# The first two w_ada sections of a hybrid decoder block: from ScalarE and GpSimd to TensorE

## The chip, the cores and the metric

The kernel runs on one NeuronCore of one Trainium2 chip. The metric is the device time of one execution in microseconds (us). Engines are named as the profile names them: PE is TensorE (PEld its weight loads), DVE is VectorE, ACT is ScalarE, POOL is GpSimd, SP the queue that issues most DMAs.

## The reference

One decoder layer on 512 tokens of width 2048, in float32, conditioned on one vector c:

```python
mod = jax.nn.silu(c) @ w_ada[l] + b_ada[l]              # (2048) @ (2048 x 12288)
sh1, sc1, g1, sh2, sc2, g2 = jnp.split(mod, 6, axis=-1)
u = _modulate(_rmsnorm(h, norm_attn[l]), sh1, sc1)      # rmsnorm(h) * (1 + sc1) + sh1
y = _hybrid_mixer(u, ...)                               # z = u @ w_in, attention, w_out
h = h + g1[:, None, :] * y
u = _modulate(_rmsnorm(h, norm_ffn[l]), sh2, sc2)
h = h + g2[:, None, :] * _swiglu(u, w_gate[l], w_up[l], w_down[l])
```

Nothing of `u @ w_in` can start for a block of channels before sh1 and sc1 of those channels are there. They are the first two of the six sections of `mod`, two products of SiLU(c) with 2048 x 2048 matrices.

## The kernel before, in words

All big products are made of pairs of fp32r numbers, high and low part, as three matmuls (`mm_ws`, L253 to L255: high by high, high by low, low by high) with 512 columns streamed. Weights come in chunks of two 128-row blocks; `fetch_w` (L221) loads one, ACT makes the high half `wh` (L237) and DVE or POOL the low half `wl` (L238).

The change lies in the early stage, the loop `while step < SLOTS + 8 or todo` (from L472). It forms sc1 and sh1 and at once uses them. The two sections are cut into 8 passes jj of 256 columns. A pass has two keys (k2 = 0 is section 1, the scale; k2 = 1 is section 0, the shift), and a key has four tiles `ad` of 512 rows by 256 columns (four row blocks q), one DMA each (L478) into 8 buffers. So there are 64 tiles, and tile n is loaded at step n. One step of the loop records, in this order: the DMA of tile `step`; the products of tile `step - 1` with SiLU(c), kept as a column per row block in `sl`; and, for the tile n that `due(step, what)` names (only the last of a pass), the sum over partitions (what = 0), `mod` and the first half of the modulation (what = 1), and its second half (what = 2). `LAGS` sets how many steps after n each comes: 3, 4 and 5, in the last pass 2, 3 and 4. Then two or three entries of `todo` are taken, each a unit of three L253 to L255 matmuls; a pass adds 14 units in the first half of the stage and 22 in the second. Each engine runs its own instructions in the recorded order.

Before the change the products of a tile are shared so: DVE multiplies and adds two or three of the four row blocks into `acc` (L490, L492), ACT multiplies the others (L497, L500), and POOL adds ACT's results into `acc2` (L501). The sum over partitions is a matmul with the 128 x 128 block of `acc` as weights and a column of ones streamed (L509), into a bank `sums`. DVE adds the bias (`mod`, L518), makes `a_vec` (L370) and `mt` (L384), ACT makes `uh` (L386), DVE makes `ul` (L390). `uh` and `ul` are what L253 to L255 stream.

In the same stage POOL makes two `wl` per pass (L238); in the second half DVE makes the `wl` for the key and value columns (index i = 1), recorded at step 2 of the next pass. DVE also computes rotary tables (L400 to L420), one instruction a step from step 6.

Of the kernel before, what the change touches and what calls it, by code (L numbers as in the profile page):

```python
# [9 lines left out]
F32 = mybir.dt.float32  # L10
F32R = mybir.dt.float32r
I32 = mybir.dt.int32
AF = mybir.ActivationFunctionType
OP = mybir.AluOpType
AX = mybir.AxisListType

P = 128
# [8 lines left out]
EPS = 1e-6  # L26
ADW = 8
LAG = 2
LAGS = (3, 4, 5), (2, 3, 4)
R_C, R_D, R_F, R_V = 1.0, 1.0, 1.0, 0.6  # L30
SCALE = HD ** -0.5
NCMP = 31
# [45 lines left out]
def hymba_block(ctx: ExitStack, tc: tile.TileContext, x, c, positions, w_ada, b_ada, norm_attn,  # L78
                norm_ffn, w_in, b_fgate, cmp_pos, w_kc1, w_kc2, w_vc1, w_vc2, beta_fox, beta_nsa,
                w_out, w_gate, w_up, w_down, final_norm, cst, out):  # L80
    nc = tc.nc
# [5 lines left out]
    def pool(stack, name, bufs=1, **kw):  # L87
        return stack.enter_context(tc.tile_pool(name=name, bufs=bufs, **kw))
# [18 lines left out]
    def bank(tag, shape=(P, T)):  # L107
        return ps.tile(list(shape), F32, tag=tag, name=uid("ps" + tag), bufs=SETS[tag])
# [6 lines left out]
    ident = cs[:, K_ID:K_ID + P]  # L115
    one_col = cs[:, K_ONE:K_ONE + 1]
# [4 lines left out]
    early = pool(st, "early")  # L121
# [23 lines left out]
    sl = con.tile([P, ND], F32, name="sl")  # L145
# [34 lines left out]
    for t in range(NT):  # L180
        for g in range(4):
# [9 lines left out]
            else:  # L191
                nc.vector.scalar_tensor_tensor(junk, src, 1.0, src, op0=OP.mult, op1=OP.mult,
                                               accum_out=ssq4[:, t, g:g + 1])
# [9 lines left out]
    b_mod = vec[:, 0:96]  # L203
# [5 lines left out]
    mod = con.tile([P, 96], F32, name="mod")  # L209
# [222 lines left out]
    NJ = ND // 2  # L432
    HJ = NJ // 2

    def w_pairs(j):
        s1 = fetch_w(p_s1, j, src=early, width=3 * P, bufs=2)
        if j < HJ:
            return [fetch_w(p_qn, j), s1]
        i = 2 * (j - HJ)
        return [fetch_w(p_cmp, i), s1, fetch_w(p_cmp, i + 1)]  # L440
# [17 lines left out]
    xsp = dram.tile([ND, P, T], F32, name="xsp")  # L458
    SLOTS = 8 * NJ

    def due(step, what):
        for n in range(7, SLOTS, 8):
            if step == n + LAGS[n == SLOTS - 1][what]:
                return n

    def on_dve(n):
        return n % 2 == 0

    tiles, accs, accs2, sums, halves, fetched, todo = {}, {}, {}, {}, {}, {}, []
    extra_work = tables()  # L470
    step = 0
    while step < SLOTS + 8 or todo:  # L472
        j, r = divmod(step, 8)
        if j < NJ:
            sec, q0 = (1, 0)[r // 4], 4 * (r % 4)
            tiles[step] = early.tile([P, 4, 256], F32, tag="adw", name=uid("ad"), bufs=ADW)
            c0 = sec * D + j * 256
            nc.sync.dma_start(tiles[step], w_ada[:, c0:c0 + 256].rearrange("(q p) n -> p q n", p=P)[:, q0:q0 + 4, :])  # L478
        if r == 2 and j < NJ:
            fetched[j] = w_pairs(j)  # L480
        n = step - 1
        if 0 <= n < SLOTS:
            key, q0 = n // 4, 4 * (n % 4)
            if q0 == 0:
                accs[key] = early.tile([P, 256], F32, tag="acc", name=uid("acc"), bufs=3)
            acc = accs[key]
            for q in (0, 1, 3) if on_dve(n) else (0, 1):
                sc1 = sl[:, q0 + q:q0 + q + 1]
                if q0 + q == 0:
                    nc.vector.tensor_scalar(acc, tiles[n][:, q, :], sc1, None, op0=OP.mult)  # L490
                else:
                    nc.vector.scalar_tensor_tensor(acc, tiles[n][:, q, :], sc1, acc, op0=OP.mult, op1=OP.add)  # L492
            for q in (2,) if on_dve(n) else (2, 3):
                sc1 = sl[:, q0 + q:q0 + q + 1]
                if q0 + q == 2:
                    accs2[key] = early.tile([P, 256], F32, tag="acc2", name=uid("acc2"), bufs=3)
                    nc.scalar.activation(accs2[key], tiles[n][:, q, :], AF.Copy, scale=sc1)  # L497
                else:
                    tm = early.tile([P, 256], F32, tag="tm", name=uid("tm"), bufs=2)
                    nc.scalar.activation(tm, tiles[n][:, q, :], AF.Copy, scale=sc1)  # L500
                    nc.gpsimd.tensor_tensor(accs2[key], accs2[key], tm, op=OP.add)  # L501
        n = due(step, 0)
        if n is not None:
            jj = n // 8
            sums[jj] = bank("mm")
            for k2 in range(2):
                for av in (accs, accs2):
                    for i in range(2):
                        nc.tensor.matmul(sums[jj][:, 2 * k2 + i:2 * k2 + i + 1],  # L509
                                         av[2 * jj + k2][:, i * P:(i + 1) * P], one_col,  # L510
                                         start=k2 == 0 and av is accs and i == 0,
                                         stop=av is accs2, skip_group_check=True)
        n = due(step, 1)
        if n is not None:
            jj = n // 8
            for k2, sec in ((0, 1), (1, 0)):
                m0 = sec * ND + 2 * jj
                nc.vector.tensor_tensor(mod[:, m0:m0 + 2], sums[jj][:, 2 * k2:2 * k2 + 2], b_mod[:, m0:m0 + 2],  # L518
                                        op=OP.add)
            scale_vec(0, jj * 2, 2)  # L520
            pend = [modulate_a(0, i, xT[:, i, :], rstd1, early) for i in (2 * jj, 2 * jj + 1)]
        n = due(step, 2)
        if n is not None:
            u.extend([modulate_b(*h) for h in pend])
            jj = n // 8
            if jj < HJ:
                todo += units(halves[jj][0], jj, S0, ND // 2)
            if jj == HJ - 1:
                todo.append(keep_half)
            todo += units(halves[jj][1], jj, S1, ND)  # L530
        for _ in range(2 if step < 8 * HJ + LAGS[0][2] else 3):
            if todo:
                todo.pop(0)()
        if 0 < j <= NJ and r % 2 == 0 and r // 2 < len(fetched[j - 1]):
            i = r // 2
            w = fetched[j - 1][i](nc.vector if i == 1 and j > HJ else nc.gpsimd)
            halves.setdefault(j - 1, []).append(w)
            pr = 2 * (j - 1 - HJ) + i // 2
            if j > HJ and i != 1:
                todo += units(w, pr, S0, ND)  # L540
        if step >= 6:
            next(extra_work, None)
        step += 1
# [378 lines left out]
    for pr in range(4):  # L922
# [4 lines left out]
        for i in range(2):  # L927
            q = pair("q", 6, "qf")
# [166 lines left out]
```

## Time and profile before

| what | value |
|---|---|
| median of three runs | 2519.67 us |
| lowest and highest run | 2519.4 and 2530.77 us |
| the profiled execution: its time, its span | 2530.77 us, 2530.7 us |
| instructions | 29434 |
| PE busy | 2408.5 us (95%), 11475 matmul records |
| DVE, ACT, POOL busy | 1253.7, 775.3, 231.9 us |
| HBM over the span | 133 GB/s |
| early stage | first 214 us of the span |

The profile lists, for the whole span and for any stretch of it, how long each engine was busy, each instruction's start and duration, what ended the idle time before it, and the TensorE clock that was granted (1.00 is 2.4 GHz, 0.50 is 1.2 GHz). A float32 matmul has two records in the trace, an fp32r matmul one; a matmul's duration includes its way through the array, so the pace of a chain is read from start to start.

### The profile page before, as it was taken

To read this page: it belongs to the slowest core of one execution; us is meant where nothing else is said; L and a number is where in the kernel's file an instruction comes from. 1 tells how busy PE (TensorE), PEld (TensorE's weight loads), DVE (VectorE), ACT (ScalarE), POOL (GpSimd) and SP (SyncE) were. 2 spreads that over 40 slices of the span, in tenths; PEclk is the share of its full clock that TensorE was granted. 3 is DMA by queue.
4 is the path that set the end of the run, shared out by engine and by line. 5 is a ranking of instruction groups with operands and counts; after the bars stand their busy time and mean duration, and the time that the engine had idled before them with its cause. 6 is when DMAs were issued, how large, how long until landed. Compare 5 with 4: busy or idle time off the path is not lost.

```text
span 2530.7 us, 29434 instructions
## 1 busy us (share of the span) xinstructions
PE 2408.5 (95%) x11475; PEld 2005.5 (79%) x11475; DVE 1253.7 (50%) x1978; ACT 775.3 (31%) x1221; POOL 231.9 (9%) x204
## 2 busy tenths in 40 slices
PE   4688999999999989999999999999999999999998
PEld 3576887788888768788888888888888888888887
DVE  8995786887755565565423323223323233322233
ACT  4443543434423332232222222222122222122233
POOL 5463000200010220000000000000000000000011
PEclk7798999999999999999999999999999999999999
DMA  9782654454644266456532333332333333233332
GB/s 301 226 275 77 187 151 125 124 156 114 189 149 150 86 206 226 149 175 191 159 100 92 100 96 96 100 94 97 100 92 100 98 93 100 96 96 100 93 99 100
DMA packets 226794, 339.02 MB, mean 134 GB/s; under 512 B 17648, under 2 KB 102480, under 8 KB 226656
## 3 DMA queue, kind: packets, MB, share of 16 engines
q1 hardware_dynamic: 223376, 332.46, 43.0%
q10 hardware_dynamic: 2304, 4.20, 0.4%
q8 instruction: 90, 1.47, 0.2%
q0 software_dynamic: 976, 0.50, 0.1%
q14 instruction: 48, 0.39, 0.1%
HBM read 324.45 MB, written 12.65 MB: 133 GB/s over the span
## 4 chain that ended last, share of the span: by engine, by line
PE 60%; DMA 2%; DVE 1%; issue 0%; ACT 0%; SPq 0%; POOLq 0%; POOL 0%; ACTq 0%; DVEq 0%
PE psmm L253 10%; PE psmm L255 10%; PE psmm L254 10%; PE pss L255 7%; PE pss L253 7%; PE pss L254 7%; PE pso L254 2%; PE pso L253 2%; PE pso L255 2%; DMA wr<-in_w_out_dram 1%; DMA ad<-in_w_ada_dram 1%; DVE acc L356 0%; DVE wl L238 0%; PE psmm L819 0%; ACT wh L237 0%
## 5 line engine op out<-in xcount | busy, mean ns | idle before, releaser
L238 DVE TENSOR_TENSOR wl<-wr,wh 128x1024 fp32r<-128x1024 f32 (+2 forms) x370 | 433.6, 1172 | 966.7 <-ACT wh L237 965.1
L237 ACT CAST wh<-wr 128x1024 fp32r<-128x1024 f32 (+2 forms) x386 | 384.5, 996 | 1199.5 <-PE pso L254 521.7
L253 PE MATMUL psmm<-uh,wh 128*128 128x512 f32 x1010 | 401.0, 398 | 11.9 <-ACT uh L386 5.7
L254 PE MATMUL psmm<-ul,wh 128*128 128x512 f32 x1010 | 398.3, 394 | 2.0 <-DVE ul L390 2.0
L255 PE MATMUL psmm<-uh,wl 128*128 128x512 f32 x1010 | 398.4, 395 | 1.3 <-DVE wl L238 1.3
L253 PE MATMUL pss<-uh,wh 128*128 128x512 f32 x600 | 238.9, 398 | 17.8 <-ACT uh L386 17.8
L254 PE MATMUL pss<-ul,wh 128*128 128x512 f32 x600 | 238.5, 398 | 5.2 <-DVE ul L390 5.2
L255 PE MATMUL pss<-uh,wl 128*128 128x512 f32 x600 | 237.9, 397 | 1.0 <-POOL wl L238 0.9
L253 PEld LDWEIGHTS psmm<-uh,wh 128*128 128x128 f32 x1010 | 192.2, 190 | 54.5 <-ACT uh L386 6.8
L356 DVE SCALAR_TENSOR_TENSOR acc<-ad,sl,acc 128x512 f32<-128x512 f32 x240 | 187.7, 782 | 94.8 <-DMA ad<-in_w_ada_dram 92.2
L255 PEld LDWEIGHTS psmm<-uh,wl 128*128 128x128 f32 x1010 | 192.4, 190 | 43.6 <-DVE wl L238 2.4
L254 PEld LDWEIGHTS psmm<-ul,wh 128*128 128x128 f32 x1010 | 192.2, 190 | 41.7 <-DVE ul L390 3.0
L992 POOL TENSOR_TENSOR fsum<-fsum,sq 128x512 f32<-128x512 f32 x13 | 19.4, 1492 | 1452.7 <-ACT sq L990 1452.0
L253 PEld LDWEIGHTS pss<-uh,wh 128*128 128x128 f32 x600 | 115.3, 192 | 43.9 <-ACT uh L386 19.7
L254 PEld LDWEIGHTS pss<-ul,wh 128*128 128x128 f32 x600 | 115.3, 192 | 31.0 <-DVE ul L390 7.0
L253 PE MATMUL psmm<-fh,wh 128*128 128x512 f32 x352 | 136.9, 389 | 0.0
L254 PE MATMUL psmm<-fl,wh 128*128 128x512 f32 x352 | 136.9, 389 | 0.0
L255 PE MATMUL psmm<-fh,wl 128*128 128x512 f32 x352 | 136.9, 389 | 0.0
L255 PEld LDWEIGHTS pss<-uh,wl 128*128 128x128 f32 x600 | 115.2, 192 | 26.0 <-POOL wl L238 1.8
L492 DVE SCALAR_TENSOR_TENSOR acc<-ad,sl,acc 128x256 f32<-128x256 f32 x144 | 111.2, 772 | 4.8 <-DMA ad<-in_w_ada_dram 0.5
L253 PE MATMUL pss<-fh,wh 128*128 128x512 f32 x264 | 102.7, 389 | 0.0
L254 PE MATMUL pss<-fl,wh 128*128 128x512 f32 x264 | 102.7, 389 | 0.0
(373 smaller groups left out, 4050.8 us busy)
## 6 DMA issues: line engine op xcount, KB each, us to landing
ad<-in_w_ada_dram SPq DMA_DIRECT2D x192, 512.0 KB, 4.4
wr<-in_w_gate_dram SPq DMA_DIRECT2D x88, 512.0 KB, 3.7
wr<-in_w_up_dram SPq DMA_DIRECT2D x88, 512.0 KB, 3.7
wr<-in_w_down_dram SPq DMA_DIRECT2D x88, 512.0 KB, 3.7
wr<-in_w_in_dram SPq DMA_DIRECT2D x104, 256.0 KB, 3.7
wr<-in_w_in_dram SPq DMA_DIRECT2D x24, 512.0 KB, 4.6
wr<-in_w_out_dram SPq DMA_DIRECT2D x24, 512.0 KB, 4.8
wr<-in_w_in_dram SPq DMA_DIRECT2D x48, 128.0 KB, 3.0
```

Source lines behind the costliest of these rows:

```text
L237: nc.scalar.copy(wh[:, :, s], v)
L238: lo.tensor_tensor(wl[:, :, s], v, split_ap(wh)[:, :, s], op=OP.subtract)
L253: nc.tensor.matmul(dst, wh[:, k, w], ah, start=first, stop=False)
L254: nc.tensor.matmul(dst, wh[:, k, w], al, start=False, stop=False)
L255: nc.tensor.matmul(dst, wl[:, k, w], ah, start=False, stop=last)
L356: nc.vector.scalar_tensor_tensor(acc, wr[:, q, :], s, acc, op0=OP.mult, op1=OP.add)
L492: nc.vector.scalar_tensor_tensor(acc, tiles[n][:, q, :], sc1, acc, op0=OP.mult, op1=OP.add)
L992: nc.gpsimd.tensor_tensor(acc[0], acc[0], sq, op=OP.add)
```

## The change

ACT and POOL no longer take part in the products. DVE keeps its share (three row blocks of an even tile, two of an odd one), and PE takes the rest: the column of `sl` is repeated to a 128 x 128 block of weights, past which 256 float32 columns of the tile are streamed (L498), so that every row of the result holds the same sums. DVE's `acc` joins by a product with a block of ones (L501). All go into one bank `rows` with two halves, used by the keys in turn. DVE multiplies each 128 columns of it with the identity and sums along the row, which picks the diagonal into a column (`dj`, L508). The sums over partitions (L509) go. `LAGS` becomes 2, 3 and 4 for every pass; the PE products are due every step, the picks after every key.

```diff
-LAGS = (3, 4, 5), (2, 3, 4)
+LAGS = 2, 3, 4
...
-    def due(step, what):
-        for n in range(7, SLOTS, 8):
-            if step == n + LAGS[n == SLOTS - 1][what]:
-                return n
-
-    def on_dve(n):
-        return n % 2 == 0
-
-    tiles, accs, accs2, sums, halves, fetched, todo = {}, {}, {}, {}, {}, {}, []
+    def due(step, what, every=8):
+        n = step - LAGS[what]
+        return n if 0 <= n < SLOTS and n % every == every - 1 else None
+
+    def n_dve(n):
+        return 3 - n % 2
+
+    tiles, accs, halves, fetched, todo = {}, {}, {}, {}, []
+    rows = bank("mm", (P, 2, 256))
+    diag = early.tile([P, 2 * NJ, 2], F32, name="diag")
...
-            for q in (0, 1, 3) if on_dve(n) else (0, 1):
+            for q in range(n_dve(n)):
...
-            for q in (2,) if on_dve(n) else (2, 3):
-                sc1 = sl[:, q0 + q:q0 + q + 1]
-                if q0 + q == 2:
-                    accs2[key] = early.tile([P, 256], F32, tag="acc2", name=uid("acc2"), bufs=3)
-                    nc.scalar.activation(accs2[key], tiles[n][:, q, :], AF.Copy, scale=sc1)
-                else:
-                    tm = early.tile([P, 256], F32, tag="tm", name=uid("tm"), bufs=2)
-                    nc.scalar.activation(tm, tiles[n][:, q, :], AF.Copy, scale=sc1)
-                    nc.gpsimd.tensor_tensor(accs2[key], accs2[key], tm, op=OP.add)
-        n = due(step, 0)
+        n = due(step, 0, 1)
         if n is not None:
-            jj = n // 8
-            sums[jj] = bank("mm")
-            for k2 in range(2):
-                for av in (accs, accs2):
-                    for i in range(2):
-                        nc.tensor.matmul(sums[jj][:, 2 * k2 + i:2 * k2 + i + 1],
-                                         av[2 * jj + k2][:, i * P:(i + 1) * P], one_col,
...
+            key, q0 = n // 4, 4 * (n % 4)
+            for q in range(n_dve(n), 4):
+                nc.tensor.matmul(rows[:, key % 2, :], sl[:, q0 + q:q0 + q + 1].to_broadcast([P, P]),
+                                 tiles[n][:, q, :], start=n % 4 == 0 and q == n_dve(n), stop=False)
+            if n % 4 == 3:
+                nc.tensor.matmul(rows[:, key % 2, :], one_col.to_broadcast([P, P]), accs[key],
+                                 start=False, stop=True)
+        n = due(step, 1, 4)
+        if n is not None:
+            key = n // 4
+            for i in range(2):
+                dj = early.tile([P, P], F32, tag="dj", name=uid("dj"), bufs=2)
+                nc.vector.scalar_tensor_tensor(dj, rows[:, key % 2, i * P:(i + 1) * P], 1.0, ident, op0=OP.mult,
+                                               op1=OP.mult, accum_out=diag[:, key, i:i + 1])
...
-                nc.vector.tensor_tensor(mod[:, m0:m0 + 2], sums[jj][:, 2 * k2:2 * k2 + 2], b_mod[:, m0:m0 + 2],
-                                        op=OP.add)
+                nc.vector.tensor_tensor(mod[:, m0:m0 + 2], diag[:, 2 * jj + k2, :], b_mod[:, m0:m0 + 2], op=OP.add)
```

How the instructions stand now, first on PE at the end of a pass in the second half of the stage. Before, the sums over partitions stand in one group, and the units follow (`pss`, `pso` and `psmm` are banks of units, `psmm` with L509 the bank `sums`):

```order
L509 MATMUL psmm_1224<-cs,acc_1008 128x1 [waits PE_49]
L509 MATMUL psmm_1224<-cs,acc_1008 128x1
L509 MATMUL psmm_1224<-cs,acc_228_1012 128x1 x2
L509 MATMUL psmm_1224<-cs,acc_1119 128x1 [waits DVE_49]
L509 MATMUL psmm_1224<-cs,acc_1119 128x1
L509 MATMUL psmm_1224<-cs,acc_253_1123 128x1 x2
L253 MATMUL pso_976<-uh_745,wh_1186 128x512
```

Now, at the same place (`psmm_286` is `rows`, `ad_908` the second tile of the next pass, `uh_947` and `ul_948` the first channels of the finished pass):

```order
L498 MATMUL psmm_286<-ad_908,sl 128x256 [waits DMAHW3_49,DVE_49]
L498 MATMUL psmm_286<-ad_908,sl 128x256
L253 MATMUL pss_872<-uh_392,wh_904 128x512
L254 MATMUL pss_872<-ul_393,wh_904 128x512
L255 MATMUL pss_872<-uh_392,wl_905 128x512
L253 MATMUL pso_873<-uh_392,wh_904 128x512
L254 MATMUL pso_873<-ul_393,wh_904 128x512
L255 MATMUL pso_873<-uh_392,wl_905 128x512
L253 MATMUL psmm_282<-uh_947,wh_964 128x512 [waits Activation_49]
L254 MATMUL psmm_282<-ul_948,wh_964 128x512 [waits DVE_49]
L255 MATMUL psmm_282<-uh_947,wl_965 128x512
L498 MATMUL psmm_286<-ad_926,sl 128x256 [waits DMAHW4_49]
```

The products of a tile now stand between the units, ahead of the units of every step, and one in four steps' products waits for DVE; the product of the first tile of that pass stands ten rows ahead of this piece, with three units between.

On DVE, the same place, before (`acc_1373` is the next pass's accumulator, `wl_1424` the low half of the key and value columns):

```order
L238 TENSOR_TENSOR wl_1424<-wr_1209,wh_1423 128x768 [waits Activation_49]
L492 SCALAR_TENSOR_TENSOR acc_1373<-ad_1388,sl,acc_1373 128x256 [waits DMAHW4_49,DVE_49]
L492 SCALAR_TENSOR_TENSOR acc_1373<-ad_1388,sl,acc_1373 128x256 [waits DVE_49] x2
L518 TENSOR_TENSOR mod<-psmm_1405,vec 128x2 [waits PE_49]
L518 TENSOR_TENSOR mod<-psmm_1405,vec 128x2
L370 SCALAR_TENSOR_TENSOR a_vec<-mod,vec 128x2 [waits DVE_49]
L384 SCALAR_TENSOR_TENSOR mt_1438<-xT,a_vec,rstd_269 128x512 [waits DVE_49]
L384 SCALAR_TENSOR_TENSOR mt_1443<-xT,a_vec,rstd_269 128x512
L492 SCALAR_TENSOR_TENSOR acc_1373<-ad_1427,sl,acc_1373 128x256 [waits DMAHW1_49]
L492 SCALAR_TENSOR_TENSOR acc_1373<-ad_1427,sl,acc_1373 128x256 [waits DVE_49]
L390 SCALAR_TENSOR_TENSOR ul_1441<-mt_1438,mod,uh_1440 128x512 [waits Activation_49]
```

And now:

```order
L508 SCALAR_TENSOR_TENSOR dj_938,diag<-psmm_286,cs 128x128 [waits PE_49]
L508 SCALAR_TENSOR_TENSOR dj_940,diag<-psmm_286,cs 128x128
L515 TENSOR_TENSOR mod<-diag,vec 128x2
L515 TENSOR_TENSOR mod<-diag,vec 128x2 [waits DVE_49]
L370 SCALAR_TENSOR_TENSOR a_vec<-mod,vec 128x2 [waits DVE_49]
L384 SCALAR_TENSOR_TENSOR mt_945<-xT,a_vec,rstd_269 128x512 [waits DVE_49]
L384 SCALAR_TENSOR_TENSOR mt_950<-xT,a_vec,rstd_269 128x512
L238 TENSOR_TENSOR wl_965<-wr_778,wh_964 128x768 [waits Activation_49]
L493 SCALAR_TENSOR_TENSOR acc_910<-ad_926,sl,acc_910 128x256 [waits DMAHW4_49]
L493 SCALAR_TENSOR_TENSOR acc_910<-ad_926,sl,acc_910 128x256 [waits DVE_49] x2
L390 SCALAR_TENSOR_TENSOR ul_948<-mt_945,mod,uh_947 128x512
```

The two picks stand ahead of `mod`, and `wl` and three instead of two products stand between `mt` and `ul`, since the modulation is recorded one step earlier while `wl` stays at its step.

## Rows read from the trace of the kernel before

**Rows 1.** The page's busy times, and a late stretch by windows (us; PEclk, DMA share, GB/s).

```profile
PE 2408.5 (95%) x11475; PEld 2005.5 (79%) x11475; DVE 1253.7 (50%) x1978; ACT 775.3 (31%) x1221; POOL 231.9 (9%) x204
...
300.00:2530.00 2230.00, 2183.99 (x10418) 1820.16 (x10416) 1008.88 (x1605) 641.56 (x974) 99.48 (x81) 0.99 0.41 123
```

**Rows 2.** Windows of the eight passes and the tail: PE, PEld, DVE, ACT, POOL busy, PEclk.

```profile
22.00:46.30 24.30, 5.97 (x24) 5.42 (x24) 22.95 (x37) 9.62 (x19) 15.05 (x15) 0.50 1.09 351
46.30:70.50 24.20, 16.53 (x58) 12.84 (x58) 23.67 (x36) 8.52 (x16) 13.95 (x12) 0.71 0.68 216
70.50:93.90 23.40, 14.70 (x58) 11.25 (x58) 22.87 (x34) 10.95 (x19) 13.56 (x12) 0.72 0.78 249
93.90:114.10 20.20, 15.09 (x58) 11.67 (x58) 19.56 (x29) 8.51 (x16) 12.89 (x12) 0.78 0.79 241
114.10:136.00 21.90, 19.16 (x72) 15.12 (x73) 20.22 (x31) 9.47 (x18) 10.67 (x11) 0.79 0.52 166
136.00:157.50 21.50, 20.44 (x93) 16.09 (x92) 20.90 (x29) 9.36 (x17) 13.44 (x12) 0.98 0.92 286
157.50:179.00 21.50, 18.79 (x82) 15.29 (x82) 20.90 (x30) 9.35 (x17) 13.41 (x12) 0.92 0.84 266
179.00:196.50 17.50, 13.06 (x60) 10.74 (x60) 15.37 (x20) 6.91 (x12) 10.96 (x9) 0.95 0.85 311
196.50:214.00 17.50, 17.50 (x66) 13.84 (x65) 8.27 (x13) 7.16 (x11) 6.67 (x4) 0.85 0.23 75
```

**Rows 3.** Groups of the early stage: line, engine, count, busy us, mean ns, idle before.

```profile
L492 DVE SCALAR_TENSOR_TENSOR acc<-ad,sl,acc 128x256 f32<-128x256 f32 x144 | 111.2, 772 | 4.8 <-DMA ad<-in_w_ada_dram 0.5
L501 POOL TENSOR_TENSOR acc<-acc,tm 128x256 f32<-128x256 f32 x80 | 68.4, 857 | 83.2 <-ACT tm L500 79.2
...
L500 ACT ACTIVATE tm<-ad,sl 128x256 f32<-128x256 f32 x80 | 38.6, 503 | 32.4 <-POOL acc L501 30.3 <-DMA ad<-in_w_ada_dram 1.7
...
L509 PE MATMUL psmm<-cs,acc 128*128 128x1 f32 x128 | 18.8, 270 | 21.2 <-DVE acc L492 20.0 <-POOL acc L501 1.2
```

**Rows 4.** Timelines of DVE and POOL, 140 to 160 us: start, us, what, count.

```profile
141.05 11.19 DVE L492 SCALAR_TENSOR_TENSOR acc<-ad,sl,acc 128x256 f32<-128x256 f32 x9
...
155.85 1.52 DVE L492 SCALAR_TENSOR_TENSOR acc<-ad,sl,acc 128x256 f32<-128x256 f32 x3
...
140.83 2.45 POOL L238 TENSOR_TENSOR wl<-wr,wh 128x1024 fp32r<-128x1024 f32 x1
143.23 4.45 POOL L501 TENSOR_TENSOR acc<-acc,tm 128x256 f32<-128x256 f32 x5
```

**Rows 5.** Timelines of PE: a unit's pace, and float32 products with a repeated column.

```profile
144.39 0.39 PE L255 MATMUL pss<-uh,wl 128*128 128x512 f32 x1
144.62 0.39 PE L253 MATMUL pss<-uh,wh 128*128 128x512 f32 x1
...
822.09 1.05 PE L171 MATMUL pss<-cs,rsnr 128*128 128x128 f32 x8
822.90 0.36 PE L258 MATMUL psmm<-wh,uh 128*128 128x256 f32 x1
```

**Rows 6.** Timeline of DVE, beginning and end of its work: a PSUM copy, the last modulation, POOL beside it.

```profile
20.22 0.28 DVE L199 COPY vec<-pss 128x128 f32<-128x128 f32 x1
...
196.31 0.23 DVE L518 TENSOR_TENSOR mod<-psmm,vec 128x2 f32<-128x2 f32 x2 [1.74 <-PE psmm L509]
...
199.63 0.96 DVE L238 TENSOR_TENSOR wl<-wr,wh 128x768 fp32r<-128x768 f32 x1 [1.51 <-ACT wh L237]
200.50 3.54 DVE L390 SCALAR_TENSOR_TENSOR ul<-mt,mod,uh 128x512 fp32r<-128x512 f32 x2
...
200.62 2.88 POOL L238 TENSOR_TENSOR wl<-wr,wh 128x1024 fp32r<-128x1024 f32 x1 [7.38 <-ACT wh L237]
```

**Rows 7.** Windows around an idle stretch of PE; columns as in rows 2.

```profile
111.80:115.80 4.00, 0.39 (x2) 0.00 (x0) 3.82 (x11) 0.77 (x2) 0.00 (x0) 1.00 0.92 287
116.40:123.20 6.80, 5.90 (x14) 4.66 (x15) 6.59 (x10) 2.74 (x7) 4.25 (x5) 0.50 0.63 211
123.20:130.00 6.80, 6.80 (x31) 5.37 (x29) 5.62 (x7) 4.85 (x9) 3.86 (x3) 1.00 0.00 0
```

More of the change, by code (lines that the diff above doesn't have):

```diff
@@ L492, in hymba_block @@
                     nc.vector.scalar_tensor_tensor(acc, tiles[n][:, q, :], sc1, acc, op0=OP.mult, op1=OP.add)
-            for q in (2,) if on_dve(n) else (2, 3):
-                sc1 = sl[:, q0 + q:q0 + q + 1]
-                if q0 + q == 2:
-                    accs2[key] = early.tile([P, 256], F32, tag="acc2", name=uid("acc2"), bufs=3)
-                    nc.scalar.activation(accs2[key], tiles[n][:, q, :], AF.Copy, scale=sc1)
-                else:
-                    tm = early.tile([P, 256], F32, tag="tm", name=uid("tm"), bufs=2)
-                    nc.scalar.activation(tm, tiles[n][:, q, :], AF.Copy, scale=sc1)
-                    nc.gpsimd.tensor_tensor(accs2[key], accs2[key], tm, op=OP.add)
-        n = due(step, 0)
-        if n is not None:
-            jj = n // 8
-            sums[jj] = bank("mm")
-            for k2 in range(2):
-                for av in (accs, accs2):
-                    for i in range(2):
-                        nc.tensor.matmul(sums[jj][:, 2 * k2 + i:2 * k2 + i + 1],
-                                         av[2 * jj + k2][:, i * P:(i + 1) * P], one_col,
-                                         start=k2 == 0 and av is accs and i == 0,
-                                         stop=av is accs2, skip_group_check=True)
+        n = due(step, 0, 1)
+        if n is not None:
+            key, q0 = n // 4, 4 * (n % 4)
[12 more added lines that the diff above has]
+                                               op1=OP.mult, accum_out=diag[:, key, i:i + 1])
         n = due(step, 1)
@@ L530, in hymba_block @@
             todo += units(halves[jj][1], jj, S1, ND)
-        for _ in range(2 if step < 8 * HJ + LAGS[0][2] else 3):
+        for _ in range(2 if step < 8 * HJ + LAGS[2] else 3):
             if todo:
```

## The prediction

> **What bounds the kernel now.** I read the page first: PE is busy for 95% of the span, and from 300 us on for 2184 of 2230 us at nearly the full clock [rows 1]. Nothing there is touched, so the change counts by how much earlier or later PE leaves the early stage, at 214 us. Then the windows, cut at the instants at which each pass gets its `mod` [rows 2]: DVE is busy for nearly all of each pass (20.90 of 21.50 us in passes 6 and 7), PE for 15 to 20 us of it, ACT for about 9, POOL for about 13. DVE is the bound of the passes; in the tail it is PE, without a gap. Then the groups: POOL idles 79 us for ACT, ACT 30 us for POOL [rows 3], so those two hand single products back and forth and neither is a bound. Last the timelines of DVE and POOL side by side [rows 4]: with POOL idle, three L492 take 1.52 us, 0.51 each; with POOL busy all the time, nine take 11.19 us. Of the 6.6 us that these nine are too long, two meet an L238 and wait some 2.0 us each; seven meet an L501 and wait 0.36 each. POOL does not slow DVE evenly, it blocks one instruction at a time.
>
> **What goes.** On ACT and POOL 80 L500 and L501 and 16 L497 go, off the path. What that gives is on DVE: 80 blocks of 0.36 us, 29 us over the stage, 3.6 us a pass. The 16 L238 of POOL stay, with some 2 us each. DVE's own products stay at 20 a pass: the words "DVE does the rest" describe the share that it had. On PE the 128 records of L509 go, 18.8 us [rows 3].
>
> **What comes.** On DVE 32 picks of 128 columns. Nearest is a copy of the same size out of PSUM, 0.28 us [rows 6]; with the sum I take 0.3, so 1.2 us a pass. Net, DVE has 2.4 us a pass less to do. On PE 96 + 16 products of 256 float32 columns. Not in the trace; nearest are four products with a repeated column as weights and 128 columns: 0.81 us from the first to what follows, 0.20 each at the full clock [rows 5]. Twice the columns make 0.41; I take 0.43, up to 0.48 for changing between the two kinds, and twice that at 1.2 GHz. A unit's matmul goes every 0.23 us [rows 5]. PE's content of a later pass, 66 matmuls and 14 products, becomes 15.2 + 6.0 = 21.2 us at the full clock, about what a pass takes now.
>
> **The new wait.** Content alone would leave the time about where it is. But PE and DVE now wait for each other in a ring, and DVE stops being the bound. The pick reads `rows`, one tile with two halves, and waits for PE. The order shows that the second tile's products in turn wait for DVE, so the halves are not treated as two buffers; the pick therefore waits for the last product recorded into the tile, the first of the next key, not only for its own key's L501. In passes 5 to 8 three units stand between those two.
>
> What the chip demands here no row before shows. The Trainium skill, PSUM — Partial Sum Buffer, section PSUM bank collisions raise a hardware error, says that TensorE and VectorE have to be kept apart by bank and quadrant, whichever columns they touch. By that rule the sum below stands; were the halves independent, leg one would begin nine matmuls and a product (2.5 us) earlier in four passes, and the sum would be 10 us smaller, 2538.
>
> From pick to pick, the ring has three legs. The counts are from the order of the changed kernel, the prices those above.
> Leg one, pick to the first `ul`, in passes 6 to 8: picks 0.6; from `mod` through `wl` 4.2, as the last pass shows it already (196.31 to where the next instruction starts, 200.50), because `wl` waits until ACT has made both `uh` and then `wh` [rows 6]; three products 1.5; one block by the L238 that ACT's next cast releases, 2.1 (200.62 in [rows 6] is such a one); `ul` itself 0.7 (half of 3.54 less that block). Together 9.1 us. PE can cover 15 matmuls and 2 products of it, 4.3 us, and idles nearly 5. In passes 2 and 3 there is no `wl` on DVE: 0.6 + 1.8 (`mod` to the end of `mt`: 199.63 less the 1.51 of waiting, less 196.31) + 0.5 for a table step, taken as a product + 1.5 + 2.1 + 0.7 = 7.2. In passes 4 and 5 no table is left and `ul` gets in ahead of the L238: 4.6.
> Leg two, PE from `ul` to the next key's pick: 18 matmuls and 5 products, 6.3 us, in passes 2 to 4; 24 and 5, 7.7, in pass 5; 20 and 5, 6.8, from pass 6.
> Leg three, to the pick that closes the pass: in passes 2 and 3 DVE is longer (picks 0.6, ten products 5.1, a block 2.1, four table steps 2.0: 9.8); in pass 4 PE (24 and 7: 8.5), in pass 5 27 and 7, 9.2, from pass 6 30 and 7, 9.9.
> Passes 2 and 3 come to 23.3 (now 24.2 and 23.4), pass 4 to 19.4 (20.2), pass 5 to 21.5 (21.9), passes 6 and 7 to 25.8 (21.5 each), pass 8, after which no tile follows, to 25.8 - 2.5 = 23.3 (17.5) [rows 2]. That is 162.4 against 150.2 us: 12.2 more.
> Pass 1, in which PE is not yet asked for units, gets shorter: 13 blocks of 0.36 go, the pick stands one step (2.5 products and a table step, 1.8 us) earlier, four picks come: -5. The tail is 66 matmuls after the last L501, 15.2 us; the first 24 cover leg one, and `mod` comes 0.9 after that L501, so 14.3 against 17.7 after `mod`: -3.4. **At the full clock the sum is +12 - 5 - 3 = +4 us.**
>
> **The clock.** PE idled for 3.6 us before 115.8, and was then granted 0.50 (1.2 GHz) for 6.8 us of nearly unbroken work, and 1.00 after that [rows 7]. Half the pace for 6.8 us costs 3.4 us. Where DVE was the bound that was free. In the ring, legs two and three are PE's, and leg one leaves it idle for 4 to 5 us in every pass. I take 3.4 us for each of seven passes, +24; the ends are nothing (the granted clock stays at 1.00) and twice that. **Forecast: +28 us.** For the profiled execution that is 2530.77 + 28 = 2559; it ran 11 us above the median of the three runs, and as the terms are differences I set them on the median: 2519.67 + 28 = **2548 us**, 2535 to 2560 for this case alone.
>
> Covers: DMA. A tile is let go by PE two steps after it landed instead of by ACT after one; eight buffers leave six steps, some 16 us, and the passes move 166 to 311 GB/s where pass 1 moved 351 [rows 2], so I cost it at nothing. Should passes fall to 16 us, DMA is late next. SP's order of loads is the same. ACT's casts come sooner.
>
> **Rivals.** *Faster: DVE relieved and PE hidden.* If leg one is covered after all (the pick never finds PE behind), passes 2 to 4 shrink by DVE's 2.4 us each, passes 5 to 7 by at most 0.7 + 0.3 + 0.3 down to PE's 21.2, pass 8 becomes 18.7 (+1.2); with -5 and -3.4 the sum is -15: 2505. For it speaks that DVE is the bound in every pass now [rows 2] and that the blocks are real [rows 4]; against it the fixed place of the picks in the order. It decides from the point where the pick finds its product done, that is where PE is under 2 us behind DVE. Chance 0.14.
> *No change: the ring without the clock.* +4, 2524; with five of the L238 blocks falling outside leg one, down to 2513. For it speaks that PE is busy for more of each pass than before; against it [rows 7]. Chance 0.24.
> *Much slower.* PE does not get back to 2.4 GHz within most passes, as in the first 46 us, where it was granted 0.50 throughout [rows 2]: twice the clock term, +52, 2572. Against it speaks that 6.8 us of work brought it back. Chance 0.10.
> The forecast keeps 0.52.
>
> **How the numbers follow.** About 0.5%, 12.6 us, is what a measurement of this kernel can tell from no change, so faster means under 2507, slower over 2532. The forecast and the much slower case are slower, 0.62; the no-change case and a small upper part of the faster one are the same, 0.26; the rest of the faster case, 0.12. The range 2510 to 2570 leaves out that rest and half of the much slower case, under 0.2 together, and holds the bounds of the product's price (0.05 x 112 = 6 us) and of the blocks.
>
> **What would show it.** L501 and L500 gone and L493 with fewer blocks, its mean from 0.77 to about 0.6 us: the relief. L498 at 0.43 from start to start at the full clock. Idle time of PE ended by `ul` (L390), once a pass, 4 us or more, and idle time of DVE ended by L498 ahead of the pick: the ring. Windows of passes 6 and 7 of 28 to 30 us with PEclk well under 1: the clock. After the early stage nothing different. I am wrong if passes 6 and 7 keep to 22 us or DVE is still busy for all of a pass; wrong on the clock alone if they take 25 to 26.

## The result and the profile after

| what | value |
|---|---|
| the changed kernel, median of 5 runs | 2541.1 us (2540.19 to 2545.69) |
| the kernel before, median of 5 runs beside it | 2521.89 us (2519.4 to 2530.77) |
| ratio | 1.0075, 95% interval 1.0056 to 1.0094 |
| profiled execution of the changed kernel, its span | 2539.6 us |
| PE leaves the early stage (end of its last unit) | 233.84 us; before 214.11 |

The change costs 19 us, 0.75%; the forecast was 28, 2548 us, with a range of 2510 to 2570. In the early stage the traces differ by 19.7 us. The profiled execution of before happened to run long in what follows the stage (2316.6 us against 2305.8), so the two spans differ by 8.9 us only; the stage's end is the better ruler, and the experiments are read by it.

First the page's busy times, then the windows of the changed kernel, cut where each pass has its `mod`; they answer to [rows 1] and [rows 2] (columns: PE, PEld, DVE, ACT, POOL busy, PEclk, DMA share, GB/s):

```profile
PE 2441.4 (96%) x11571; PEld 2034.7 (80%) x11571; DVE 1224.9 (48%) x2042; ACT 733.7 (29%) x1125; POOL 165.6 (7%) x124
```

```profile
22.00:38.30 16.30, 10.09 (x38) 7.69 (x38) 15.40 (x40) 1.53 (x2) 2.35 (x1) 0.90 1.09 360
38.30:62.10 23.80, 19.41 (x70) 15.04 (x70) 20.09 (x44) 3.05 (x4) 4.67 (x2) 0.78 0.97 309
62.10:86.00 23.90, 19.16 (x70) 14.95 (x70) 19.99 (x45) 5.60 (x7) 4.66 (x2) 0.86 0.68 217
86.00:106.90 20.90, 18.15 (x70) 14.19 (x70) 16.67 (x38) 3.05 (x4) 5.00 (x2) 0.92 0.84 272
106.90:129.90 23.00, 20.67 (x82) 16.59 (x83) 16.83 (x38) 4.22 (x6) 4.61 (x2) 0.93 0.63 193
129.90:160.00 30.10, 23.86 (x96) 19.32 (x95) 17.87 (x37) 4.00 (x5) 5.04 (x2) 0.89 0.72 231
160.00:190.50 30.50, 24.18 (x96) 19.59 (x95) 17.99 (x39) 4.00 (x5) 5.11 (x2) 0.89 0.57 179
190.50:218.50 28.00, 21.75 (x84) 17.59 (x83) 15.67 (x34) 4.00 (x5) 5.04 (x2) 0.88 0.42 160
218.50:233.80 15.30, 14.81 (x64) 11.49 (x62) 8.62 (x16) 7.25 (x11) 6.78 (x5) 1.00 0.28 93
```

The loss is in one place. Passes 2 to 5 take 91.6 us against 89.7, pass 1 is 7.8 us shorter, the tail 2.5 shorter; passes 6, 7 and 8 take 88.5 us against 60.5. In them neither DVE (18 of 30 us) nor PE (24 of 30) is busy all the time: the bound is gone, and waiting has come. The views of the waits of PE and DVE, 38 to 236 us (us in total, times, longest), say for whom:

```profile
PE psmm L254 <- DVE ul L390: 19.3, 4, 6.3
PE pss L254 <- DVE ul L390: 9.5, 4, 3.4
```

```profile
DVE dj L508 <- PE psmm L498: 42.3, 13, 6.0
DVE dj L508 <- PE psmm L501: 4.4, 1, 4.4
```

PE waits for `ul`, and DVE's picks wait for PE, for L498 and not for the L501 that completes their key. The timeline of DVE shows a whole leg, from pick to `ul` at the beginning of pass 7, then those of POOL and PE at the same time:

```profile
159.61 0.29 DVE L508 SCALAR_TENSOR_TENSOR dj<-psmm,cs 128x128 f32<-128x128 f32 x1 [4.60 <-PE psmm L498]
...
160.43 1.41 DVE L384 SCALAR_TENSOR_TENSOR mt<-xT,a_vec,rstd 128x512 f32<-128x512 f32 x2
163.42 0.96 DVE L238 TENSOR_TENSOR wl<-wr,wh 128x768 fp32r<-128x768 f32 x1 [1.58 <-ACT wh L237]
164.30 5.44 DVE L493 SCALAR_TENSOR_TENSOR acc<-ad,sl,acc 128x256 f32<-128x256 f32 x3
169.66 1.40 DVE L390 SCALAR_TENSOR_TENSOR ul<-mt,mod,uh 128x512 fp32r<-128x512 f32 x2
```

```profile
164.35 5.11 POOL L238 TENSOR_TENSOR wl<-wr,wh 128x1024 fp32r<-128x1024 f32 x2 [25.09 <-ACT wh L237]
```

```profile
163.75 0.40 PE L253 MATMUL psmm<-uh,wh 128*128 128x512 f32 x1
170.46 0.79 PE L254 MATMUL psmm<-ul,wh 128*128 128x512 f32 x1 [6.32 <-DVE ul L390]
```

DVE waits 1.58 us for ACT, makes `wl` in 0.96, and starts three products just as POOL starts two L238: they take 5.44 us, where three alone take 1.52 [rows 4]. That is 3.9 us for two blocks. The Trainium skill, SBUF — State Buffer, section Who interferes with whom, calls the port that VectorE and GpSimd share an exclusive lock, held for a whole instruction; these rows agree, with 3.9 us lost by DVE beside the 5.11 us of POOL's two instructions.

The prices of the products can be read in PE's timeline. Two of L498 (four records) go in 0.67 us, and the unit behind them needs 0.42 instead of 0.23 from start to start, so 0.86 us for two; and in the groups L493 has come from a mean of 772 ns [rows 3] to 599:

```profile
54.31 1.02 PE L498 MATMUL psmm<-ad,sl 128*128 128x256 f32 x4
54.98 0.58 PE L253 MATMUL psmm<-uh,wh 128*128 128x512 f32 x1
55.40 0.39 PE L254 MATMUL psmm<-ul,wh 128*128 128x512 f32 x1
```

```profile
L493 DVE SCALAR_TENSOR_TENSOR acc<-ad,sl,acc 128x256 f32<-128x256 f32 x144 | 86.3, 599 | 4.3 <-DMA ad<-in_w_ada_dram 0.2
```

### The profile page after: what moved, and what is told of

Same layout as the page of the kernel before. It is cut to its first block, busy times and chain, and to the rows that moved or that the text cites. A ratio compares the mean times of both kernels' runs of the same rounds, so it can differ in the third digit from the quotient of the medians.

```text
span 2539.6 us, 29411 instructions
## 1 busy us (share of the span) xinstructions
PE 2441.4 (96%) x11571; PEld 2034.7 (80%) x11571; DVE 1224.9 (48%) x2042; ACT 733.7 (29%) x1125; POOL 165.6 (7%) x124
## 4 chain that ended last, share of the span: by engine, by line
PE 62%; DMA 1%; DVE 1%; ACT 0%; issue 0%; POOLq 0%; POOL 0%; SPq 0%; ACTq 0%; DVEq 0%
PE psmm L255 10%; PE psmm L253 10%; PE psmm L254 10%; PE pss L253 8%; PE pss L254 8%; PE pss L255 8%; PE pso L255 2%; PE pso L253 2%; PE pso L254 2%; DMA ad<-in_w_ada_dram 0%; DMA wr<-in_w_out_dram 0%; PE psmm L815 0%; DMA out_dram<-ot 0%; PE pss L360 0%; DVE wl L238 0%
## 5 line engine op out<-in xcount | busy, mean ns | idle before, releaser
L238 DVE TENSOR_TENSOR wl<-wr,wh 128x1024 fp32r<-128x1024 f32 (+2 forms) x370 | 434.1, 1173 | 972.2 <-ACT wh L237 970.3
L254 PEld LDWEIGHTS psmm<-ul,wh 128*128 128x128 f32 x1010 | 193.0, 191 | 59.9 <-DVE ul L390 21.2
L255 PE MATMUL pss<-fh,wl 128*128 128x512 f32 x264 | 102.7, 389 | 0.0
```

What stands on the lines that cost most here:

```text
L238: lo.tensor_tensor(wl[:, :, s], v, split_ap(wh)[:, :, s], op=OP.subtract)
L254: nc.tensor.matmul(dst, wh[:, k, w], al, start=False, stop=False)
L255: nc.tensor.matmul(dst, wl[:, k, w], ah, start=False, stop=last)
```

## The experiments

Theory A is the prediction's: DVE and PE wait for each other, and the legs of that ring set the time. B: TensorE has simply been given too much. C: the lower clock after each idle stretch is a large part. The results in one table; a pass ends at its `mod`, "PE leaves" is the end of its last unit, "slow clock" the time between 38 us and that end with the granted clock at 0.50, and each ratio is to the kernel before on the same chip (its median there: 2528.1 us for e1 to e4, 2527.5 for e5 to e8, 2525.1 for e9 to e11).

| kernel | passes 2 to 5, us | passes 6 to 8, us | PE leaves | slow clock | median | ratio, 95% interval |
|---|---|---|---|---|---|---|
| before | 24.2 23.4 20.2 21.9 | 21.5 21.5 17.5 | 214.1 | 64.7 | | |
| changed | 23.9 23.8 20.9 23.0 | 30.1 30.4 28.0 | 233.8 | 44.4 | 2541.1 | 1.0075 (1.0056 to 1.0094) |
| e1_no_ring | 20.5 20.2 17.1 19.2 | 19.9 20.2 15.6 | 199.0 | 17.1 | 2511.5 | 0.9941 (0.9923 to 0.9960) |
| e2_pick_first | 22.0 21.9 19.9 19.1 | 27.0 27.1 27.0 | 217.2 | 17.1 | 2527.6 | 1.0006 (0.9990 to 1.0021) |
| e3_wl_first | 22.8 23.3 20.9 22.8 | 23.4 23.4 20.9 | 210.0 | 20.5 | 2522.2 | 0.9983 (0.9974 to 0.9992) |
| e4_warm | 23.9 22.0 20.8 21.4 | 28.0 28.0 25.4 | 222.6 | 10.2 | 2533.8 | 1.0027 (1.0014 to 1.0039) |
| e5_both | 22.2 21.9 19.9 19.9 | 21.2 21.3 21.3 | 199.9 | 10.2 | 2512.0 | 0.9944 (0.9931 to 0.9958) |
| e6_both_dve | 22.8 21.7 22.6 23.1 | 21.2 21.3 21.3 | 206.7 | 20.5 | 2518.6 | 0.9975 (0.9960 to 0.9991) |
| e7_old_lags | 22.3 21.0 20.4 23.9 | 23.0 23.0 20.5 | 208.3 | 20.2 | 2518.9 | 0.9967 (0.9950 to 0.9984) |
| e8_relief | 19.8 19.1 16.4 18.8 | 17.7 17.7 13.9 | 180.3 | 29.2 | 2492.0 | 0.9869 (0.9836 to 0.9902) |
| e9_all_first | 19.5 18.7 19.1 19.0 | 21.2 21.3 21.3 | 193.6 | 6.8 | 2505.0 | 0.9911 (0.9890 to 0.9932) |
| e10_spread | 18.8 18.7 17.5 19.0 | 21.2 21.3 21.3 | 191.9 | 3.4 | 2501.4 | 0.9904 (0.9883 to 0.9925) |
| e11_after_again | 24.1 24.0 21.0 23.0 | 30.2 30.5 28.0 | 234.2 | 47.8 | 2540.7 | 1.0061 (1.0041 to 1.0080) |

**e1_no_ring**, the picks without the wait for PE; they read a piece of `xT`, which leaves the sums out of `mod`:

```diff
-nc.vector.scalar_tensor_tensor(dj, rows[:, key % 2, i * P:(i + 1) * P], 1.0, ident, ...
+nc.vector.scalar_tensor_tensor(dj, xT[:, 2 * (key // 2) + i, 0:P], 1.0, ident, ...
```

> The picks read a piece of xT instead of the bank rows, so that mod no longer depends on TensorE; all products, picks and units stay. This leaves the sums out of mod, so its numbers are not the reference's. Theory A (the ring: DVE and PE wait for each other): PE then only runs through its own content, from 44 us on some 432 unit matmuls of 0.23 and 96 products of 0.43 = 140 us, a little more where DVE's passes of 18 to 20 us are longer than PE's; PE leaves the early stage at 190 to 200 us instead of 233.8, the time is 2495 to 2510 us. Theory B (PE is simply given too much: 48 us of products more than it had): PE was short of time anyway, the stage still ends at 225 to 235 us, the time is 2533 to 2542 us.

PE left at 199.0 us, 35 us sooner than in the changed kernel, with every product, pick and unit in place; the time missed the upper end of A's 2495 to 2510 by 1.5 us. B falls: the added work fits into less time than the kernel before needed.

**e2_pick_first**, the seven lines of the picks ahead of those of the PE products, in the same step:

```diff
+        n = due(step, 1, 4)
+        ...
         n = due(step, 0, 1)
         ...
-        n = due(step, 1, 4)
-        ...
```

> The picks of a key are recorded ahead of the product of the next key's first tile, in the same step; nothing else changes. Theory A with the one-bank wait as its long leg: the pick now waits for its own key's L501 only and starts 2.0 to 2.5 us earlier against it, DVE's idle time ahead of the picks of passes 6 and 7 falls from 5.5 and 4.6 to about 3 and 2 us, each of passes 2 to 8 shortens by 1.5 to 2.5 us (two picks lie on it, only one ahead of mod), the early stage ends at 217 to 224 us, the time is 2524 to 2532 us. Theory B (too much on PE) or a ring whose long leg is elsewhere: no change, 2538 to 2544 us. Other way: PE now waits for the pick at the first product of each key, 0.6 us each, and gives 16 x 0.6 = 10 us back; then 2535 to 2542 us.

PE left at 217.2, 16.6 us sooner, and the time, 2527.6, lies in A's range. Waiting for the next key's product was a real leg of the ring. The passes became 1.0 to 3.9 us shorter, not evenly 1.5 to 2.5. DVE's waits ahead of the picks fell from 46.7 to 28.6 us over the stage, though 4.6 us stayed in pass 6, more than the 3 expected; what PE spends waiting for picks is 3.6 us in all, against 4.0 in the changed kernel. The picks are L499 here, and their waits end with L508, the product that completes their own key:

```profile
DVE dj L499 <- PE psmm L508: 28.6, 9, 6.9
PE psmm L505 <- DVE dj L499: 3.6, 4, 1.4
```

A part of the 16.6 us is the clock: the time at 0.50 fell from 44.4 to 17.1 us with the waits. The Trainium skill, PSUM — Partial Sum Buffer, section PSUM bank collisions raise a hardware error, tells of a compiler's scheduler that puts a dependency between any two instructions of different engines on one bank and quadrant. Both keys share one bank here; the wait of the pick for L498 in the changed kernel agrees with that. No run gives each key a tile or a bank of its own, so which of the two this program keeps apart is not shown.

**e3_wl_first**, the `wl` that DVE makes in each of passes 6 to 8 and in the tail moved from the end of its step to the beginning:

```diff
+        if r == 2 and HJ < j <= NJ:
+            halves[j - 1].append(fetched[j - 1][1](nc.vector))
         n = step - 1
...
-        if 0 < j <= NJ and r % 2 == 0 and r // 2 < len(fetched[j - 1]):
+        if not (r == 2 and j > HJ) and 0 < j <= NJ and r % 2 == 0 and r // 2 < len(fetched[j - 1]):
```

> The low half of the key and value columns (L238 on DVE, from pass 5 on) is recorded at the beginning of its step, ahead of the products, the picks and mod, as it stood ahead of mod in the kernel before. Theory A: it leaves the leg from pick to ul, with its wait 1.51 and its 0.96 us; PE's idle time ended by ul in passes 6, 7 and 8 falls from 6.25 to about 3.8 us, the stage ends 5 to 8 us earlier, the time is 2533 to 2536 us. If the wait for ACT just moves with it, or the L238 of POOL fall elsewhere: within 2 us of 2541.

The expectation was far too low. PE left 23.8 us sooner, at 210.0, sooner than in the kernel before. Passes 6 to 8 became 6.7 to 7.1 us shorter each, not 2.5. DVE's timeline after `mod` and POOL's and PE's beside it show why:

```profile
152.87 1.52 DVE L495 SCALAR_TENSOR_TENSOR acc<-ad,sl,acc 128x256 f32<-128x256 f32 x3
154.30 3.55 DVE L390 SCALAR_TENSOR_TENSOR ul<-mt,mod,uh 128x512 fp32r<-128x512 f32 x2
```

```profile
154.72 5.35 POOL L238 TENSOR_TENSOR wl<-wr,wh 128x1024 fp32r<-128x1024 f32 x2 [18.06 <-ACT wh L237]
```

```profile
154.85 0.40 PE L253 MATMUL psmm<-uh,wh 128*128 128x512 f32 x1
155.10 0.51 PE L254 MATMUL psmm<-ul,wh 128*128 128x512 f32 x1
```

Without the 2.5 us of `wl` and its wait the three products (1.52) are through and the first `ul` has begun before POOL's first L238 starts, at 154.72; the block falls on the second `ul`. Two blocks of 2 us leave the leg with it, PE does not idle at all there, and its clock stays at 1.00. One instruction of 0.96 us in the wrong place cost some 7 us a pass.

**e4_warm**, filler products with zero weights where PE idles:

```diff
+    fill = {1: 15, 2: 8, 3: 8, 4: 24, 5: 24, 6: 24}
...
+            for _ in range(n):
+                nc.tensor.matmul(dst, zw, u[0][0], start=False, stop=False)
```

> Ahead of the first unit of passes 2 to 7 PE gets filler matmuls with zero weights that add nothing to a sum: 15, 8, 8, 24, 24 and 24, each 0.23 us at the full clock, which is 3.5, 1.8, 1.8 and 5.5 us, a little under the idle time there. Theory C (a good part of the loss is the lower clock after each idle stretch): the granted clock stays at 1.00 behind ul; after these six stretches PE now spends 1.6 to 3 us each at half pace too long, 14 us in all; the stage ends at 219 to 224 us, the time is 2526 to 2532 us. My prediction's price of 3.4 us for each would give 20 us: 2521. If DVE has the longer leg after ul anyway, or the clock falls all the same: 2538 to 2543 us.

(The expectation counts passes by their units, which run in passes 3 to 8 of the table.) Windows around the idle stretch of pass 6, of the changed kernel and then of e4_warm:

```profile
133.90:140.20 6.30, 0.12 (x1) 0.00 (x0) 6.23 (x6) 1.19 (x2) 5.04 (x2) 0.86 0.50 160
140.20:147.00 6.80, 6.74 (x20) 5.45 (x21) 3.75 (x9) 0.00 (x0) 0.00 (x0) 0.63 0.50 141
147.00:153.80 6.80, 6.80 (x31) 5.61 (x30) 3.91 (x12) 0.00 (x0) 0.00 (x0) 1.00 0.89 307
```

```profile
127.00:134.00 7.00, 7.00 (x33) 5.77 (x32) 5.41 (x6) 4.01 (x5) 3.82 (x2) 1.00 0.97 305
134.00:140.80 6.80, 5.89 (x27) 4.62 (x26) 6.07 (x10) 0.00 (x0) 1.38 (x1) 1.00 0.30 94
140.80:147.60 6.80, 6.80 (x32) 5.60 (x31) 3.92 (x12) 0.00 (x0) 0.00 (x0) 1.00 1.03 328
```

With PE kept busy the granted clock stays at 1.00 (2.4 GHz) from 49.2 us to the end of the stage. PE leaves 11.2 us sooner, and passes 3 to 8 make 10.6 of it: C is right in kind, but at 1.8 us for each of the six instead of 3.4; the time, 2533.8, missed its range by 2 us. The other 8.5 us of the stage's loss stay with the clock at 1.00 from pass 3 on: that much the clock does not explain there.

**e5_both**, the edits of e2_pick_first and e3_wl_first together.

> The edits of the two runs before together: the picks ahead of the next key's product, and the low half of the key and value columns at the beginning of its step. Theory A: the two take different pieces of the same leg, so passes 6 to 8 are left with PE's own content, 66 x 0.23 + 14 x 0.43 = 21.2 us, up to 22.5; passes 2 to 5 stay at the 22.0, 21.9, 19.9 and 19.1 us that the first edit gave. PE leaves the early stage at 200 to 204 us, the time is 2508 to 2516 us. If the two pay for the same waiting (either alone was enough): 208 to 211 us and 2519 to 2523 us.

It came as A said: PE left at 199.9, as early as with no ring at all (199.0). The windows of passes 7 and 8 show PE busy without a gap:

```profile
142.70:164.00 21.30, 21.30 (x96) 17.73 (x95) 17.99 (x37) 4.11 (x5) 5.06 (x2) 1.00 0.84 264
164.00:185.30 21.30, 21.30 (x96) 17.73 (x95) 15.88 (x34) 4.11 (x5) 5.06 (x2) 1.00 0.65 231
```

21.3 us is the content that the prediction gave PE, 66 x 0.23 + 14 x 0.43 = 21.2. The ring is still in the program; in passes 6 to 8 its legs are now covered.

**e6_both_dve**, all low halves on DVE:

```diff
-            w = fetched[j - 1][i](nc.vector if i == 1 and j > HJ else nc.gpsimd)
+            w = fetched[j - 1][i](nc.vector)
```

> As e5_both, and all low halves of the early stage (L238) on DVE, none on POOL, so that nothing blocks DVE: 16 instructions of 0.96 and 1.2 us come to DVE, two a pass, and 16 blocks of some 2 us go. Theory A with POOL's blocks in the leg from pick to ul: two ul take 1.4 us in every pass instead of 5.1, 5.1, 3.0, 3.0 and 3.5, PE's idle time ended by ul in passes 1 to 5 (3.1 to 3.4, and 1.5 us) all but goes, and PE leaves the stage 5 to 10 us earlier than in e5_both; 2500 to 2508 us. If DVE now waits for ACT's casts in its own order, or was hidden there: within 2 us of e5_both.

A miss: 206.7, 6.8 us later than e5_both. Passes 4 and 5 take 2.7 and 3.2 us longer than in e5_both, passes 2 and 3 0.6 longer and 0.2 shorter. DVE's timeline of pass 4 shows the trap of e3 again, now in the first half of the stage, where the edit had left this `wl` at the end of its step:

```profile
83.10 1.42 DVE L384 SCALAR_TENSOR_TENSOR mt<-xT,a_vec,rstd 128x512 f32<-128x512 f32 x2
86.03 0.96 DVE L238 TENSOR_TENSOR wl<-wr,wh 128x768 fp32r<-128x768 f32 x1 [1.51 <-ACT wh L237]
86.90 1.52 DVE L495 SCALAR_TENSOR_TENSOR acc<-ad,sl,acc 128x256 f32<-128x256 f32 x3
```

In passes 2 and 3 a block ahead of the first `ul` is gone, and 2.5 us of `wl` with its wait stand in its place. In passes 4 and 5 they come on top: in e5_both's pass 4 POOL's L238 started at 85.14 us, when the first `ul` had begun at 84.94, so that no block was there to save.

**e7_old_lags**, one part of the change undone, with `wl` where it was:

```diff
-LAGS = 2, 3, 4
+LAGS = 3, 4, 5
```

> One part of the change undone: LAGS back at 3, 4 and 5 (for all passes), so that products, picks, mod and ul come one step later, and the low half of the key and value columns stands a step ahead of mod again, without being moved itself. Theory A: as in e3_wl_first PE's idle time of 6.25 us in passes 6, 7 and 8 goes, passes 6 and 7 take 23 to 24 us; the last pass ends one step (2 to 3 us) later; PE leaves the stage at 211 to 216 us instead of 233.8, the time is 2521 to 2527 us. If the step of wl is not what stretches those passes: 2538 to 2545 us.

PE left at 208.3, a little before the range. The steps alone, with the bank's wait and all the new products in place, decide over 25 us: with `mod` one step later, `wl` stands ahead of it again.

**e8_relief**, the kernel before without the work of ACT and POOL and with nothing for it on PE:

```diff
-            for q in (2,) if on_dve(n) else (2, 3):
-                ...
-                for av in (accs, accs2):
+                for av in (accs,):
```

> The kernel before, without the shares of ACT and POOL (L497, L500, L501 and their half of L509), and nothing in their place: sc1 and sh1 are summed over DVE's row blocks alone. It shows what the removal alone is worth to DVE. My prediction took 80 blocks of 0.36 us, 3.6 us a pass: the stage ends 22 to 29 us earlier than in the kernel before, at 186 to 192 us instead of 214, unless PE, with 15 to 17 us of units a pass, or the DMA is late next; 2494 to 2502 us. If DVE's blocks were hidden by other waiting: 2515 to 2528 us.

Each of passes 2 to 8 became 3.1 to 4.4 us shorter, 26.8 in sum, pass 1 4.7, the tail 2.4; PE left at 180.3, earlier than expected, and the time, 2492, is just below the range. The group of its products, by line:

```profile
L492 DVE SCALAR_TENSOR_TENSOR acc<-ad,sl,acc 128x256 f32<-128x256 f32 x144 | 84.1, 584 | 4.3
```

So the relief is real and as large as predicted. What the change offers is that; what it pays, besides waits, is PE's 21.3 us in passes 6 to 8 where DVE would now do 17.7.

**e9_all_first**, as e6_both_dve with this `wl` first in every pass:

```diff
-        if r == 2 and HJ < j <= NJ:
+        if r == 2 and 0 < j <= NJ:
```

> As e6_both_dve, but in every pass, not only from pass 5 on, the second low half (wl) stands at the beginning of its step, so that none is left between mt and ul. Theory A: what made e6_both_dve slower than e5_both is the same place of wl, now in passes 2 to 5 (DVE waits 1.51 us for ACT and works 0.96 there); with it gone PE's idle time ended by ul in passes 2 and 3 falls from 3.4 us to 1 or less, passes 2 to 5 take 78 to 81 us in sum against 83.9 in e5_both and 90.2 in e6_both_dve, passes 6 to 8 stay at 21.3. PE leaves the stage at 195 to 198 us, the time is 2505 to 2509 us. If DVE loses the time by having the low halves at all: 205 us or later, 2516 or more.

193.6 us, a little before the range, and 2505.0: passes 2 to 5 take 76.3 us, also less than expected. So e6's loss was the place of `wl`, not DVE's having the low halves.

**e10_spread**, one unit kept for the step of `mod`:

```diff
-        for _ in range(2 if step < 8 * HJ + LAGS[2] else 3):
+        for _ in range((1 if r in (1, 2) else 2) if step < 8 * HJ + LAGS[2] else 3):
```

> As e9_all_first, and in the first half of the stage the 14 units of a pass are spread over all eight steps (2, 1, 1 and then 2 each) so that PE still has one in the step in which mod is formed. Theory A: it covers 0.7 us more of the leg from pick to ul; 0 to 2 us less than e9_all_first. Rival: the last units come later, so the next pick does too, and it is 0 to 2 us more.

191.9 us, 1.7 sooner, as A expected; the times of the two (2505.0 and 2501.4) have overlapping intervals. Its windows of passes 4 to 7:

```profile
77.00:94.50 17.50, 16.03 (x70) 13.06 (x70) 14.91 (x38) 3.06 (x4) 0.00 (x0) 1.00 0.93 293
94.50:113.60 19.10, 17.78 (x79) 14.46 (x78) 16.30 (x42) 4.24 (x6) 0.00 (x0) 1.00 0.73 217
113.60:134.70 21.10, 21.10 (x95) 17.60 (x94) 16.01 (x39) 4.11 (x5) 0.00 (x0) 1.00 0.99 318
134.70:156.00 21.30, 21.30 (x96) 17.76 (x95) 16.10 (x39) 4.11 (x5) 0.00 (x0) 1.00 0.85 269
```

PE is busy for over 90% of a pass of the first half and for all of one in the second. This kernel does all the new products on PE and is 1.0% faster than the kernel before (0.9883 to 0.9925), and so faster than both.

**e11_after_again**, the changed kernel unaltered.

> The changed kernel once more, beside the kernel before on the same chip, since the kernel before ranged from 2517 to 2536 us over these runs: the early stage ends at 233 to 235 us as in its first profile, and the time is 2540 to 2545 us, 12 to 18 us above the median of the kernel before.

The stage ended at 234.2, the median was 2540.7 beside 2525.08 of the kernel before, 15.6 us. The kernel before ranged from 2517.2 to 2535.5 us over all runs, so its median in five of them is uncertain by some us; the two ratios, 1.0075 and 1.0061, agree within their intervals.

## Why the prediction was right, and where it was not

The sign, the place and the ring held; the split between the ring and the clock did not. Its sum, against what the trace of the changed kernel shows for the same stretches:

| stretch | predicted | measured |
|---|---|---|
| pass 1 | -5 | -7.8 |
| passes 2 to 5: legs, and 4 x 3.4 of clock | 87.5 + 13.6 - 89.7 = +11.4 | 91.6 - 89.7 = +1.9 |
| passes 6 to 8: legs, and 3 x 3.4 of clock | 74.9 + 10.2 - 60.5 = +24.6 | 88.5 - 60.5 = +28.0 |
| tail | -3.4 | -2.5 |
| sum | +28 | +19.6 |

- **The relief.** 3.6 us a pass was predicted, e8_relief, from which half of L509 is gone too, shows 3.1 to 4.4; L493 came to 599 ns where "about 0.6 us" was said.
- **The price of a product,** 0.43 us at the full clock, was right: e5_both's passes at 21.3 us, with PE busy throughout, are that content.
- **The wait of the pick for the next key's first product** was right. The prediction put 10 us on it, in four passes at the full clock; e2_pick_first gave 16.6 with what the clock gave back, and the same edit on top of e3_wl_first 10.1 (e5_both). It shortened passes 2 and 3 of the changed kernel too, by 1.9 us each, which that figure left out.
- **Leg one in passes 6 to 8** was predicted with `wl` in it, PE idling "nearly 5" us; it idled 6.3. The mis-sized term is POOL's block: one of 2.1 us was counted, two fall there (5.44 us for three products). Nor did the prediction see that they fall there only because `wl` holds the products back until POOL starts; e3_wl_first showed it. In e4_warm, with the clock at 1.00, passes 3 to 5 take 64.2 us, as much in sum as their predicted legs (single passes are off by up to 1.4), and passes 6 to 8 81.4 against 74.9: the legs that were too short are those of passes 6 to 8.
- **The clock.** This is the term that was most mis-sized: 3.4 us for each of seven passes, +24, where e4_warm recovered 10.6 us in six. The first step that failed is "half the pace for 6.8 us costs 3.4 us". In passes 6 to 8 the clock falls while PE still idles: in pass 6 the windows give 0.86 before `ul` (1.8 us of 6.3 at 0.50) and 0.63 behind it (5.0 of 6.8), so work meets 5 us of it, 2.5 us of loss; in passes 7 and 8 1.3 and 0.9 us fall on idle time, and e4_warm shortened the three passes by 2.1, 2.4 and 2.6. The second is that passes 4 and 5, where PE waits 1.5 us only for `ul`, got a share like the others. The clock was at 0.50 for 3.4 us there, not 6.8, and e4_warm gave 0.1 and 1.6 us. In the first of them PE, now at the full clock, comes to the product that completes the key (L512 there) ahead of DVE and waits, which the changed kernel's PE does not have to:

```profile
92.88 0.70 PE L512 MATMUL psmm<-acc,cs 128*128 128x256 f32 x2 [1.18 <-DVE acc L504]
```

- **Pass 1** was 2.8 us better than said. In e7_old_lags, with the old steps, its `mod` comes 3.4 us later than in the changed kernel (41.7 to 38.3), so the step that the pick moved was worth 3.4 us, not 1.8; the other 1.2 us are open.
- **The rivals.** "The ring without the clock" priced the ring at +4; with the clock at 1.00 it was +8.5 (e4_warm). "Faster: DVE relieved and PE hidden" had the condition that the pick finds its product done or nearly so and leg one is covered. In the changed kernel that fails. In e5_both it is brought about in passes 6 to 8 by order alone, in e9_all_first and e10_spread nearly throughout, with POOL's low halves also moved to DVE, and the time goes to 2512, 2505 and 2501 us, around the 2505 that it gave. "Much slower" did not come: in passes 3 to 8 PEclk is 0.86 to 0.93, so each low stretch ended within its pass. Its "first 46 us" were misread: [rows 2] begin at 22 us, and over the 22 us before the granted clock was 0.97.

The errors of passes 2 to 5 and of passes 6 to 8 have opposite signs, so the sum is nearer to the truth than its terms, and that much of its being right is luck. What stays open is how the remaining PE wait for `ul` in e10_spread (5.1 us over four passes) could be covered.

## What to carry to other kernels

Where work moves from an engine that was the bound to one that was not, look at what the bound had hidden: here one 0.96 us instruction between `mt` and `ul` was free while DVE was always busy, and cost 7 us a pass once PE waited for `ul`. Before blaming the moved work, list each engine's order between the two ends of every wait that goes both ways, and take out of it whatever could stand elsewhere. Two keys in one tile and one PSUM bank were one buffer to this program; record the reader of the first ahead of the writer of the second.

## What had not been expected of the hardware

That the granted clock can fall before PE resumes, so that a part of the slow stretch costs nothing (1.8 us of it in pass 6; none in passes 4 and 5, where it fell at 90.6 and 111.1 us, 0.7 and 0.2 us after PE had resumed), the prediction did not expect. Nor did it think of filler products: 24 of them, 5.5 us by their count, held the clock at 1.00 and with it returned 2.1 us in pass 6, although PE still idled for 0.9 us behind them until `ul` was there.
